# First ConvGLU tiles: where products, low parts, raw weights and one PSUM bank are placed

## The chip, the cores and the metric

The kernel runs on one core of a Trainium2 chip. Its time is the device time of one launch in microseconds (us), and a kernel's time is the median of several launches.

## The reference, cut to what matters

One layer: S5 scan and chunked attention, an output projection, then the channel mixer (ConvGLU), which is what the change is about. 512 prompt frames and 8 x 16 sample frames make T = 640 columns; D_MODEL is 1024, D_FF is 2816.

```python
h = x + mix @ p['w_o']                       # output projection, residual
hn = rms_norm(h, p['g_ffn'])
up = hn @ p['w_up']                          # 1024 -> 2 * 2816
a, b = jnp.split(up, [D_FF], axis=-1)        # gate half and value half
c, new_conv = causal_depthwise_conv(a, conv_hist, p['conv_w'], p['conv_b'])   # width 3
out = h + (jax.nn.gelu(c) * b) @ p['w_down'] # 2816 -> 1024
```

## The kernel before

Everything is fp32, and the columns lie along the free dimension (tiles of 128 x 640). For each product of a weight and an activation the kernel keeps both as a high part (rounded to fp32r, TensorE's fast format) and a low part (the rest), and adds high x high, high x low and low x high in PSUM.

The ConvGLU starts about 480 us into the program and lasts to the end. It works on 22 tiles `f` of 128 gate and 128 value columns, in parts of 2, 4, 4, 4, 4 and 4 tiles (`PARTS`). A tile's up-projection is written as seven products on halves of the matrices (in the manner of Strassen): A11, s1, s2, A12, s3, A22, s4, where A are quarters of the weights and s are sums of quarters (`PRODUCTS`). A product has two segments of six matmuls of 128x320 each. The seven products share four PSUM banks: A11 and A12 write sS, s1 writes sP, s2 and A22 write sT, s3 and s4 write sX. So three products wait until what lay in their bank has been read: A12 for ScalarE's copy `u2 <- sS` (L1454, `u` in the trace), A22 for VectorE's sum of `u2` and sT (L1456), and s4 for VectorE's sum of sX and `u2` (L1458). VectorE then takes the gate from sT (L1356 to L1358), the convolution (L1365, L1367), ScalarE the GELU (L1370, L1371), VectorE the product of gate and value (L1380); ScalarE copies its high part (L1381) and VectorE subtracts for its low part (L1384).

From the second part on, each tile is followed by segments of the down-projection for the tiles of the part before (four of them for f = 2 to 5, eight from f = 6 on), and VectorE adds each of their results to the residual `h_` (`down_evac`, L1407). The up-projection is fed with h without its norm: the factor 1/rms (`RS`) multiplies the gate (L1357, L1358), and since the value half is not multiplied, the residual h itself is multiplied by rms (`RM`) tile by tile (L1489, eight times), so that all that is added to it has the same factor. At the very end the final norm takes the factor out again.

The weights of tile f are two raw loads of 512 KB on the SP queue: "1" (A11 and A12) and "2" (A21 and A22); a third load "d" holds down-projection weights. All three take turns in a ring of three buffers (`wr`). VectorE makes the sums (`sums_a`, L1316 and L1317, from "2" and "1"; `sums_b`, L1322 and L1323). `parts` then makes high and low parts: ScalarE writes minus the raw values into the low tile (L1297) and rounds the raw values into the high tile (L1298), whose rounding is the same with the sign turned, and GpSimd issues a DMA that adds the raw values onto the low tile (L1299). That accumulating DMA takes the sums `s` and `t` from the chip's own memory, but "a" (from "1") and "d" a second time from HBM (argument `again`). A22's parts (`gh`, `gl`) are made by ScalarE and VectorE (L1305, L1310).

The order on each engine is written out by hand: `at(position, fn)` puts work in front of the segment with that number, `prep` holds the positions for each tile, `q` is the number of the tile's first segment and `qp` that of the tile before. Each engine runs its own instructions in that order; SP's queue holds the raw loads, GpSimd's the accumulating DMAs. Positions below zero lie in the output projection before the ConvGLU, whose own weights are split by ScalarE (`wh`, L107) and VectorE (`wl`, L112).

The ends of two lists that the change touches:

```python
A.activation(lo, src, AF.Copy, scale=-1.0)
A.activation(hi, src, AF.Copy)
G.dma_start(lo, src if again is None else again, accum_op=OP.add)
...
for i in range(8):
    at((20, 26, 34, 40, 48, 54, 62, 68)[i], lambda i=i: V.tensor_tensor(h_[i], h_[i], RM, op=OP.mult))
```

Of the kernel before, what the change touches and what calls it, by code (L numbers as in the profile page):

```python
# [24 lines left out]
PARTS = (2, 4, 4, 4, 4, 4)  # L25
# [6 lines left out]
U_D = [U_F + 44]  # L32
# [11 lines left out]
def body(nc, tc, d, ctx):  # L44
# [8 lines left out]
    V, A, G, PE, S = nc.vector, nc.scalar, nc.gpsimd, nc.tensor, nc.sync  # L53
# [27 lines left out]
    RS = const.tile([128, T], F32, name="RS")  # L81
# [980 lines left out]
    n = 0  # L1062
# [32 lines left out]
    for i in range(8):  # L1095
        if i in (2, 4, 5, 6):
            p = pair()
            a = att[(2, 4, 5, 6).index(i)]
# [41 lines left out]
    h_, X = [None] * 8, [None] * 4  # L1140
# [19 lines left out]
    def mid():  # L1160
        return h2.tile([128, T], F32, tag="m", name=nm("m"), bufs=4)
# [105 lines left out]
    R = {}  # L1267
    ops = {}
    held = {}

    def load_raw(key, u, cols=slice(0, 1024)):
        if key in (("1", 0), ("2", 0)):

            R[key] = tmp[:, 1024 * (key[0] == "2"):][:, 0:1024]
            S.dma_start(R[key], d["w"][u])
            return
        n = cols.stop - cols.start
        R[key] = wp.tile([128, 1024], F32, tag="wr", bufs=3, name=nm("wr"))[:, 0:n]
        S.dma_start(R[key], d["w"][u, :, cols])

    RING = {"w": (wp, "wh", "wl", 1024, 2), "f": (wf, "fh", "fl", 1024, 2)}

    def parts(ring, key, src, again=None):

        if ring == "m":

            t = [mid().bitcast(F32R)[:, 0:512] for _ in range(4)]
            for i in range(2):
                A.activation(t[2 + i], src[:, 512 * i:512 * i + 512], AF.Copy, scale=-1.0)
                A.activation(t[i], src[:, 512 * i:512 * i + 512], AF.Copy)  # L1290
                G.dma_start(t[2 + i], src[:, 512 * i:512 * i + 512], accum_op=OP.add)
            ops[key] = [(t[0], t[2]), (t[1], t[3])]
            return
        pool, th, tl, width, bufs = RING[ring]
        n = src.shape[-1]
        hi, lo = (pool.tile([128, width], F32R, tag=t, name=nm(t), bufs=bufs)[:, 0:n] for t in (th, tl))
        A.activation(lo, src, AF.Copy, scale=-1.0)  # L1297
        A.activation(hi, src, AF.Copy)  # L1298
        G.dma_start(lo, src if again is None else again, accum_op=OP.add)  # L1299
        ops[key] = [(hi[:, c:c + 512], lo[:, c:c + 512]) for c in range(0, n, 512)]  # L1300

    def parts_g(f):
# [8 lines left out]

    ssum = {}

    def sums_a(f):
        t = fp.tile([128, 1024], F32, tag="sa", name=nm("s"), bufs=1)
        V.tensor_tensor(t[:, 0:512], R["2", f][:, 0:512], R["2", f][:, 512:1024], op=OP.add)  # L1316
        V.tensor_tensor(t[:, 512:1024], t[:, 0:512], R["1", f][:, 0:512], op=OP.add)  # L1317
        ssum["s", f] = t

    def sums_b(f):  # L1320
        t = fp.tile([128, 1024], F32, tag="sb", name=nm("s"), bufs=1)
        V.tensor_tensor(t[:, 0:512], R["1", f][:, 0:512], R["2", f][:, 0:512], op=OP.add)  # L1322
        V.tensor_tensor(t[:, 512:1024], ssum["s", f][:, 512:1024], R["1", f][:, 512:1024], op=OP.add)  # L1323
        ssum["t", f] = t


# [7 lines left out]
    def up_seg(f, n, half):  # L1334
        w, x, b = PRODUCTS[n]
        if half == 0:
            held[b] = smps(b)
        ps = held[b][:, :HT]
        kind, part = HOME[w]
        hi, lo = ops[kind, f][part]  # L1340
        for k in (2 * half, 2 * half + 1):
            xh_, xl_ = X[k][x]
            c = slice(128 * k, 128 * k + 128)
            mm(ps, hi[:, c], xh_, k == 0, False)
            mm(ps, hi[:, c], xl_, False, False)
            mm(ps, lo[:, c], xh_, False, k == 3)
# [22 lines left out]
    def gelu():  # L1369
        A.activation(g_t[:, 0:512], c_t[:, 0:512], AF.Gelu_apprx_tanh)  # L1370
        A.activation(g_t[:, 512:640].rearrange("p (n i) -> p n i", n=NS), c_sample(c_t), AF.Gelu_apprx_tanh)  # L1371

    cs = {}

    def product(f, j):
        if j < 3:
            cs[f] = (ht(F32R), ht(F32R))
        else:
            cs[f] = tuple(h2.tile([128, T], F32R, tag="m", name=nm("m"), bufs=4) for _ in range(2))
        V.tensor_tensor(g_t, g_t, b_t, op=OP.mult)  # L1380
        A.activation(cs[f][0], g_t, AF.Copy)  # L1381

    def product_lo(f):
        V.tensor_tensor(cs[f][1], g_t, cs[f][0].bitcast(F32), op=OP.subtract)  # L1384

    downs = {}

# [18 lines left out]
    def down_evac(i):  # L1406
        V.tensor_tensor(two(h_[i]), downs[i][:, :, :HT], two(h_[i]), op=OP.add)  # L1407
# [2 lines left out]

    def prep(f, q, qp):
        if f == 0:
            p = (-61, -59, -46, -44, (-42, "f"), (-36, "f"), (-8, "w"), -30, -28)
        elif f == 1:
            p = (-29, -21, -12, 8, (6, "m"), (3, "w"), (10, "f"), 12, 13)
        elif f == 2:
            p = (5, 7, 15, 20, (17, "f"), (14, "w"), (22, "m"), 26, 28)
        elif f == 3:
            p = (24, 30, 35, 37, (37, "f"), (36, "w"), (42, "f"), 40, 42)
        else:  # L1420
            e = q - qp > 18
            p = (qp - 4, qp - 2, qp + 4, qp + 6, (qp + 6, "f"), (qp + 8, "w"), (qp + (17 if e else 14), "f"),
                 qp + 12, qp + (17 if e else 13))
        u = U_F + 2 * f
        at(p[0], lambda: load_raw(("1", f), u))
        at(p[1], lambda: load_raw(("2", f), u + 1))
        at(p[2], lambda: sums_a(f))
        at(p[3], lambda: sums_b(f))
        at(p[4][0], lambda: parts(p[4][1], ("s", f), ssum["s", f]))
        at(p[5][0], lambda: parts(p[5][1], ("a", f), R["1", f], d["w"][u]))  # L1430
        at(p[6][0], lambda: parts(p[6][1], ("t", f), ssum["t", f]))
        at(p[7], lambda: parts_g(f))
        at(p[8], lambda: parts_g_lo(f))

    f0, prev, qp = 0, None, 0
    for p, nf in enumerate(PARTS):
        for j in range(nf):
            f = f0 + j
            q = len(segs)
            prep(f, q, qp)  # L1440
            qp = q
# [20 lines left out]
            e = q + 2 * (f == 0)  # L1462
# [38 lines left out]

# [7 lines left out]
    segs = ((0, SEG_A), (SEG_A, T))  # L1509
# [227 lines left out]
```

## Time and profile before

| | |
|---|---|
| median of 3 runs | 934.83 us (933.84 to 936.38) |
| profiled execution, its own time | 934.26 us |
| span of that execution, first to last instruction | 932.4 us |
| mean granted TensorE clock | 0.995 |
| busy: PE, DVE, ACT, POOL | 97 %, 67 %, 47 %, 14 % |
| SP queue's loads (hardware DMA) | 33.8 % of the 16 DMA engines' span |
| GpSimd's DMAs (software DMA) | 30.7 % |

The profile is of one execution. PE is TensorE, DVE is VectorE, ACT is ScalarE, POOL is GpSimd and SP is the queue that issues loads. L115 is the one line that issues nearly all matmuls, so its groups are told apart by their tiles: sS, sP, sT and sX are the four banks of the up-projection, pb the larger banks of the down-projection and of the output projection. An idle time in brackets is that of the engine just before the row, with the instruction that ended it.

### The profile page before, as it was taken

Reading aid. Unit: us, or ns where it says so; the run is one execution under the profiler, and the core shown is the slowest. Engines: PE = TensorE matmul, PEld = TensorE weight load, DVE = VectorE, ACT = ScalarE, POOL = GpSimd, SP = SyncE. Lnnn points to the kernel's source line nnn. Section 1 sums busy time; section 2 is a strip of 40 time slices with the busy share of each in tenths; the row PEclk is TensorE's granted clock in tenths of the full one; section 3 lists DMA queues with packets and bytes.
Section 4 is the critical chain, followed back from the end, with each engine's and each line's share of the span. In section 5 each row is a group of like instructions: output and inputs, shape, how many; then the busy total and the mean of one; then the engine's idle time right before and its main releaser. Section 6 shows DMA issues by size and latency. Waiting matters only on the chain.

```text
span 932.4 us, 16524 instructions
## 1 busy us (share of the span) xinstructions
PE 903.9 (97%) x6534; PEld 867.4 (93%) x6534; DVE 627.6 (67%) x1261; ACT 441.5 (47%) x689; POOL 135.1 (14%) x230
## 2 busy tenths in 40 slices
PE   8999999999999999999998999999999999999995
PEld 7978999987878899999998899999999999999994
DVE  6793997376676444486777887666666666667545
ACT  7144112354343554434675555544646446454531
POOL 0111402400000000000012222221222212121200
PEclk9999999999999999999999999999999999999998
DMA  6744328777566422244457689888888888898833
GB/s 228 196 147 128 116 89 69 205 241 256 172 210 209 119 88 87 72 155 122 131 107 174 142 186 207 202 188 195 186 183 202 190 190 188 184 202 189 187 55 113
DMA packets 62428, 151.76 MB, mean 163 GB/s; under 512 B 20944, under 2 KB 24208, under 8 KB 62352
## 3 DMA queue, kind: packets, MB, share of 16 engines
q1 hardware_dynamic: 45392, 95.90, 33.8%
q0 software_dynamic: 16096, 54.03, 30.7%
q8 instruction: 51, 0.84, 0.4%
q10 hardware_dynamic: 864, 0.78, 0.3%
q14 instruction: 25, 0.20, 0.1%
HBM read 114.56 MB, written 8.21 MB: 132 GB/s over the span
## 4 chain that ended last, share of the span: by engine, by line
PE 73%; DVE 10%; ACT 6%; DMA 5%; issue 4%; POOL 1%; SPq 0%; DVEq 0%; POOLq 0%; ACTq 0%
PE pb L115 40%; PE sS L115 9%; PE sT L115 8%; PE sX L115 7%; PE sP L115 5%; DMA wl<-in_w 3%; DMA o_s<-SV 2%; PE sT L746 1%; PE sX L822 1%; DVE h L1535 1%; ACT wh L107 1%; PE sS L794 1%; DVE wl L112 1%; DVE h L1209 1%; DVE sm L271 1%
## 5 line engine op out<-in xcount | busy, mean ns | idle before, releaser
L115 PE MATMUL pb<-h,wh 128*128 128x320 f32 (+2 forms) x2000 | 383.5, 312 | 5.1 <-ACT h L955 1.5
L115 PEld LDWEIGHTS pb<-h,wh 128*128 128x128 f32 x2000 | 312.4, 188 | 11.0 <-issue 3.3
L115 PE MATMUL pb<-h,wl 128*128 128x320 f32 (+2 forms) x1000 | 230.1, 309 | 0.4 <-DVE wl L112 0.4
L115 PEld LDWEIGHTS pb<-h,wl 128*128 128x128 f32 x1000 | 167.3, 188 | 0.9 <-DVE wl L112 0.7
L1299 POOL DMA_DIRECT2D fl<-s x41 | 35.8, 874 | 432.9 <-PE pb L115 251.9
L107 ACT ACTIVATE wh<-wr 128x1024 fp32r<-128x1024 f32 x50 | 52.7, 1054 | 80.4 <-PE pb L115 59.9
L112 DVE TENSOR_TENSOR wl<-wr,wh 128x1024 fp32r<-128x1024 f32 x50 | 61.1, 1222 | 39.5 <-ACT wh L107 39.4
L115 PE MATMUL sS<-h,wh 128*128 128x320 f32 x336 | 74.7, 309 | 0.0
L115 PE MATMUL sX<-h,fh 128*128 128x320 f32 x320 | 71.3, 310 | 0.0
L1297 ACT ACTIVATE fl<-s 128x1024 fp32r<-128x1024 f32 x41 | 43.3, 1057 | 55.2 <-PE sT L115 48.3
L115 PEld LDWEIGHTS sS<-h,wh 128*128 128x128 f32 x336 | 56.2, 188 | 0.0
L115 PE MATMUL sS<-h,wl 128*128 128x320 f32 x168 | 52.2, 311 | 2.9 <-DMA wl<-in_w 2.9
L115 PEld LDWEIGHTS sX<-h,fh 128*128 128x128 f32 x320 | 53.8, 189 | 0.0
L693 ACT ACTIVATE sb<-sb,mx 128x128 f32<-128x128 f32 (+4 forms) x40 | 24.2, 604 | 57.7 <-DVE mx L692 44.2
L1299 POOL DMA_DIRECT2D wl<-in_w x43 | 38.2, 889 | 86.3 <-ACT wl L1297 79.1
L1370 ACT ACTIVATE tmp<-tmp 128x512 f32<-128x512 f32 x22 | 13.9, 633 | 76.4 <-DVE tmp L1367 76.4
L115 PE MATMUL sX<-h,fl 128*128 128x320 f32 x160 | 49.5, 309 | 0.0
L1297 ACT ACTIVATE wl<-wr 128x1024 fp32r<-128x1024 f32 (+1 forms) x43 | 43.5, 1011 | 6.8 <-PE sS L115 5.7
L115 PE MATMUL sT<-h,gh 128*128 128x320 f32 x176 | 40.4, 317 | 4.9 <-DVE u L1456 4.9
L1298 ACT ACTIVATE wh<-wr 128x1024 fp32r<-128x1024 f32 (+1 forms) x43 | 43.2, 1004 | 0.0
L1298 ACT ACTIVATE fh<-s 128x1024 fp32r<-128x1024 f32 x41 | 42.9, 1046 | 0.0
L1367 DVE SCALAR_TENSOR_TENSOR tmp<-tmp,vec 128x656 f32<-128x656 f32 x44 | 39.5, 898 | 0.7
(339 smaller groups left out, 1678.3 us busy)
## 6 DMA issues: line engine op xcount, KB each, us to landing
wr<-in_w SPq DMA_DIRECT2D x112, 512.0 KB, 4.6
fl<-s POOLq DMA_DIRECT2D x41, 512.0 KB, 6.0
wl<-in_w POOLq DMA_DIRECT2D x39, 512.0 KB, 8.4
kc<-in_kc SPq DMA_DIRECT2D x16, 512.0 KB, 5.4
vc<-in_vc SPq DMA_DIRECT2D x16, 512.0 KB, 5.6
x<-in_x SPq DMA_DIRECT2D x7, 320.0 KB, 6.1
pb<-in_pbias SPq DMA_DIRECT2D x8, 256.0 KB, 5.9
h<-in_x SPq DMA_DIRECT2D x6, 320.0 KB, 4.2
```

The lines of the kernel that those rows point to most:

```text
L107: A.activation(hi, raws[u], AF.Copy)
L112: V.tensor_tensor(lo, raws[u], hi.bitcast(F32), op=OP.subtract)
L115: PE.matmul(ps, lhs, rhs, start=start, stop=stop)
L271: ops.append((cost, lambda: f(*a, **k)))
L693: A.activation(sb[:, :w], sb[:, :w], AF.Exp, bias=mx[:, 2:3], accum_out=mx[:, 3:4])
L746: PE.transpose(pt[:, k * 128:k * 128 + 128], e[:, k * 128:k * 128 + 128], ident)
L794: PE.matmul(sc[32 * n:32 * n + 32, :], QB[:, hp, 4 * g4 + n].rearrange("p a b -> p (a b)"), kc[n // 2][:, n % 2, :], start=True, stop=True ...
L1297: A.activation(lo, src, AF.Copy, scale=-1.0)
L1298: A.activation(hi, src, AF.Copy)
L1299: G.dma_start(lo, src if again is None else again, accum_op=OP.add)
L1367: V.scalar_tensor_tensor(c_t, a_t[:, j:L + j], vcol(C_CW + 3 * f + j), c_t, op0=OP.mult, op1=OP.add)
L1370: A.activation(g_t[:, 0:512], c_t[:, 0:512], AF.Gelu_apprx_tanh)
```

## The change

- `parts` no longer takes a source in HBM: every accumulating DMA reads the raw tile or the sum that ScalarE has read. With `cuts` it works in pieces; "a" of f = 3, 4, 5 is made in two halves, each with a DMA of its own.
- The raw tile "1" of f = 4 and 5 is loaded as two halves into buffers of another pool (`mid`, which holds the `m` tiles), not into the ring.
- For f = 0 and 1, A22 writes a bank of the larger kind (`bigps`, pb in the trace), not sT.
- The products of f = 0 to 5 are multiplied by RS on VectorE. The eight multiplications of h by RM move into the third part (f = 6 to 9), each three segments behind the `down_evac` of the same tile of h.
- For f = 2 to 5 the product's low part is made by a ScalarE copy with scale -1 and an accumulating DMA, in place of VectorE's subtraction.
- Positions: product and its low part one and two segments later; loads, sums and parts of f = 0, 3, 4, 5 and, by one segment, the load "1" from f = 6 on.

```diff
+        if key in (("1", 4), ("1", 5)):
+            R[key] = [mid()[:, 0:512] for _ in range(2)]
+            for i in range(2):
+                S.dma_start(R[key][i], d["w"][u, :, 512 * i:512 * i + 512])
+            return
...
-    def parts(ring, key, src, again=None):
+    def parts(ring, key, src, cuts=1):
...
-        A.activation(lo, src, AF.Copy, scale=-1.0)
-        A.activation(hi, src, AF.Copy)
-        G.dma_start(lo, src if again is None else again, accum_op=OP.add)
+        for c in (slice(i, i + n // cuts) for i in range(0, n, n // cuts)):
+            x = src[c.start // 512] if isinstance(src, list) else src[:, c]
+            A.activation(lo[:, c], x, AF.Copy, scale=-1.0)
+            A.activation(hi[:, c], x, AF.Copy)
+            G.dma_start(lo[:, c], x, accum_op=OP.add)
...
-            held[b] = smps(b)
+            held[b] = bigps()[:, 0] if w == "A22" and f < 2 else smps(b)
...
+    EARLY = sum(PARTS[:2])
...
         V.tensor_tensor(g_t, g_t, b_t, op=OP.mult)
+        if f < EARLY:
+            V.tensor_tensor(g_t, g_t, RS, op=OP.mult)
+        if 1 < f < EARLY:
+            A.activation(cs[f][1], g_t, AF.Copy, scale=-1.0)
         A.activation(cs[f][0], g_t, AF.Copy)
+        if 1 < f < EARLY:
+            G.dma_start(cs[f][1], g_t, accum_op=OP.add)
 
     def product_lo(f):
-        V.tensor_tensor(cs[f][1], g_t, cs[f][0].bitcast(F32), op=OP.subtract)
+        if not 1 < f < EARLY:
+            V.tensor_tensor(cs[f][1], g_t, cs[f][0].bitcast(F32), op=OP.subtract)
...
-            p = (-61, -59, -46, -44, (-42, "f"), (-36, "f"), (-8, "w"), -30, -28)
+            p = (-61, -59, -50, -44, (-44, "f"), (-54, "f"), (-8, "w"), -30, -28)
...
-            p = (24, 30, 35, 37, (37, "f"), (36, "w"), (42, "f"), 40, 42)
+            p = (24, 30, 35, 38, (38, "f"), (36, "w"), (42, "f"), 40, 42)
...
-            p = (qp - 4, qp - 2, qp + 4, qp + 6, (qp + 6, "f"), (qp + 8, "w"), (qp + (17 if e else 14), "f"),
+            p = (qp - 3, qp - 2, qp + 4, qp + 6, (qp + 6, "f"), (qp + 8, "w"), (qp + (17 if e else 14), "f"),
                  qp + 12, qp + (17 if e else 13))
+            if f < 6:
+                p = (43 if f == 4 else 54, 44 if f == 4 else 58) + p[2:]
...
-        at(p[5][0], lambda: parts(p[5][1], ("a", f), R["1", f], d["w"][u]))
+        at(p[5][0], lambda: parts(p[5][1], ("a", f), R["1", f], 2 if 2 < f < 6 else 1))
...
-            at(e + 17, lambda f=f, j=j: product(f, j))
-            at(e + 18, lambda f=f: product_lo(f))
+            at(e + 18, lambda f=f, j=j: product(f, j))
+            at(e + 20, lambda f=f: product_lo(f))
...
+                    if p == 2:
+                        at(len(segs) + 3, lambda i=i: V.tensor_tensor(h_[i], h_[i], RM, op=OP.mult))
...
-    for i in range(8):
-        at((20, 26, 34, 40, 48, 54, 62, 68)[i], lambda i=i: V.tensor_tensor(h_[i], h_[i], RM, op=OP.mult))
```

Three places show what moves. Line numbers from 1274 on are shifted in the changed program: L1380 becomes L1392, L1384 L1403, L1322 L1333, L1323 L1334, L1455 L1476, L1456 L1477, L1458 L1479, L1454 L1475, L1381 L1397, L1297 L1304 and L1298 L1305. First VectorE behind the GELU of f = 0, while TensorE works on f = 1; before:

```order
L1380 TENSOR_TENSOR tmp<-tmp 128x640
L1384 TENSOR_TENSOR h_5529<-tmp,h_5528 128x640
L1322 TENSOR_TENSOR s_5539<-wr_5352,wr_5377 128x512
L1323 TENSOR_TENSOR s_5539<-s_5481,wr_5352 128x512
L1489 TENSOR_TENSOR h_4735<-h_4735,RM 128x640
L1455 TENSOR_TENSOR tmp<-sS_5545,u_4663 128x320
L1456 TENSOR_TENSOR u_4663<-sT_5521,u_4663 128x320
L1458 TENSOR_TENSOR tmp<-sX_5570,u_4663 128x320
```

and in the changed program:

```order
L1392 TENSOR_TENSOR tmp<-tmp 128x640
L1394 TENSOR_TENSOR tmp<-tmp,RS 128x640
L1333 TENSOR_TENSOR s_5539<-wr_5352,wr_5377 128x512
L1334 TENSOR_TENSOR s_5539<-s_5481,wr_5352 128x512
L1403 TENSOR_TENSOR h_5535<-tmp,h_5534 128x640
L1476 TENSOR_TENSOR tmp<-sS_5544,u_4663 128x320
L1477 TENSOR_TENSOR u_4663<-sT_5521,u_4663 128x320
L1479 TENSOR_TENSOR tmp<-sX_5570,u_4663 128x320
```

One multiplication stands for another (RS for RM), and the low part (L1403) has gone from the second place to behind the sums.

Second ScalarE between the GELU of f = 2 and the copy that frees bank sS for A12 of f = 3; before:

```order
L1370 ACTIVATE tmp<-tmp 128x512
L1371 ACTIVATE tmp<-tmp 128x128
L1381 ACTIVATE h_5806<-tmp 128x640
L1297 ACTIVATE wl_5826<-wr_5738 128x512
L1298 ACTIVATE wh_5825<-wr_5738 128x512
L1454 ACTIVATE u_4663<-sS_5818 128x320
```

and in the changed program:

```order
L1381 ACTIVATE tmp<-tmp 128x512
L1382 ACTIVATE tmp<-tmp 128x128
L1396 ACTIVATE h_5816<-tmp 128x640
L1397 ACTIVATE h_5815<-tmp 128x640
L1304 ACTIVATE wl_5831<-wr_5740 128x512
L1305 ACTIVATE wh_5830<-wr_5740 128x512
L1475 ACTIVATE u_4663<-sS_5823 128x320
```

One copy (L1396, the one with scale -1) has come in ahead of it.

Third the SP queue, the three raw loads ("d", "1", "2") that are issued in one tile from f = 7 on, with the semaphores that each waits for (DMASW are those of GpSimd's DMAs, DMAHW those of the loads before it); before:

```order
L1279 DMA wr_6494<-in_w 128x1024 [waits DMAHW0_49,Activation_49]
L1279 DMA wr_6528<-in_w 128x1024 [waits DMAHW1_49,DVE_49,Activation_49]
L1279 DMA wr_6543<-in_w 128x1024 [waits DMAHW2_49,DVE_49,Activation_49]
```

and in the changed program:

```order
L1284 DMA wr_6509<-in_w 128x1024 [waits DMAHW2_49,DMASW0_49,Activation_49]
L1284 DMA wr_6549<-in_w 128x1024 [waits DMASW2_49,DMAHW3_49,DVE_49,Activation_49]
L1284 DMA wr_6558<-in_w 128x1024 [waits DMAHW4_49,DVE_49]
```

"d" and "1" now wait for one of GpSimd's accumulating DMAs as well; "2" does not.

## Rows read from the trace of the kernel before

**Rows 1.** By stretch: length, busy PE, PEld, DVE, ACT, POOL, clock, DMA share, GB/s.

```profile
500.00:520.00 20.00, 16.02 (x97) 15.76 (x98) 15.91 (x28) 9.78 (x15) 5.77 (x9) 0.91 0.54 122
...
580.00:620.00 40.00, 40.00 (x275) 40.00 (x274) 27.96 (x46) 22.05 (x29) 9.07 (x15) 1.00 0.83 188
```

**Rows 2.** What PE waited for, 440 to 932 us: total, times, longest.

```profile
PE sT L115 <- DVE u L1456: 4.9, 3, 2.9
PE sS L115 <- DMA wl<-in_w: 2.9, 3, 2.0
...
PE pb L115 <- DVE h L1407: 0.8, 1, 0.8
PE pb L115 <- ACT wh L107: 0.6, 1, 0.6
...
PE pb L115 <- DVE wl L112: 0.4, 1, 0.4
```

**Rows 3.** Timeline of ACT in the output projection: start, length, idle before.

```profile
431.64 0.83 ACT L1197 ACTIVATE m<-h,vec 128x640 f32<-128x640 f32 x1 [3.54 <-DVE h L1209]
...
443.83 1.05 ACT L1297 ACTIVATE fl<-tmp 128x1024 fp32r<-128x1024 f32 x1
...
448.07 0.83 ACT L1197 ACTIVATE m<-h,vec 128x640 f32<-128x640 f32 x1 [1.62 <-DVE h L1209]
```

**Rows 4.** Timeline of DVE, 497 to 503 us (f = 1).

```profile
497.37 0.83 DVE L1380 TENSOR_TENSOR tmp<-tmp 128x640 f32<-128x640 f32 x1 [2.57 <-ACT tmp L1371]
499.00 0.82 DVE L1384 TENSOR_TENSOR h<-tmp,h 128x640 fp32r<-128x640 f32 x1 [0.81 <-ACT h L1381]
...
502.80 0.49 DVE L1458 TENSOR_TENSOR tmp<-sX,u 128x320 f32<-128x320 f32 x1
```

**Rows 5.** Timeline of PE, 499 to 506 us (f = 1: end of s3, A22, s4).

```profile
499.55 0.31 PE L115 MATMUL sX<-h,fl 128*128 128x320 f32 x1
...
502.75 0.68 PE L115 MATMUL sT<-h,gh 128*128 128x320 f32 x2 [2.89 <-DVE u L1456]
...
505.89 0.72 PE L115 MATMUL sX<-h,fh 128*128 128x320 f32 x2
```

**Rows 6.** Timelines of ACT and of PE at A12 of f = 3.

```profile
529.49 0.42 ACT L1454 ACTIVATE u<-sS 128x320 f32<-128x320 f32 x1
...
530.53 0.46 PE L115 MATMUL sS<-h,wh 128*128 128x320 f32 x2
```

**Rows 7.** DMA issues of 580 to 880 us: number, KB, median us to landing.

```profile
wr<-in_w SPq DMA_DIRECT2D x47, 512.0 KB, 7.8
wl<-in_w POOLq DMA_DIRECT2D x32, 512.0 KB, 8.7
fl<-s POOLq DMA_DIRECT2D x30, 512.0 KB, 5.8
```

**Rows 8.** DMAs issued at 598.5, 599.2 and 614.5 us.

```profile
wl<-in_w POOLq DMA_DIRECT2D x1, 512.0 KB, 10.5
wr<-in_w SPq DMA_DIRECT2D x1, 512.0 KB, 10.0
...
wr<-in_w SPq DMA_DIRECT2D x1, 512.0 KB, 3.6
```

**Rows 9.** One tile in the steady run, 605 to 626 us: POOL, DVE and PE.

```profile
605.68 0.88 POOL L1299 DMA_DIRECT2D wl<-in_w  x1 [1.03 <-ACT wl L1297]
...
613.77 0.69 DVE L1310 TENSOR_TENSOR gl<-wr,gh 128x512 fp32r<-128x512 f32 x1
...
618.24 0.69 DVE L1316 TENSOR_TENSOR s<-wr 128x512 f32<-128x512 f32 x1 [0.92 <-DMA wr<-in_w]
...
621.12 0.69 DVE L1322 TENSOR_TENSOR s<-wr,wr 128x512 f32<-128x512 f32 x1 [1.46 <-DMA fl<-s]
...
623.61 0.49 DVE L1455 TENSOR_TENSOR tmp<-sS,u 128x320 f32<-128x320 f32 x1 [1.19 <-PE sS L115]
...
625.10 0.46 PE L115 MATMUL sT<-h,gh 128*128 128x320 f32 x2
```

More of the change, by code (lines that the diff above doesn't have):

```diff
@@ L1294, in parts @@
         pool, th, tl, width, bufs = RING[ring]
-        n = src.shape[-1]
+        n = 1024 if isinstance(src, list) else src.shape[-1]
         hi, lo = (pool.tile([128, width], F32R, tag=t, name=nm(t), bufs=bufs)[:, 0:n] for t in (th, tl))
-        A.activation(lo, src, AF.Copy, scale=-1.0)
-        A.activation(hi, src, AF.Copy)
-        G.dma_start(lo, src if again is None else again, accum_op=OP.add)
+        for c in (slice(i, i + n // cuts) for i in range(0, n, n // cuts)):
[3 more added lines that the diff above has]
+            G.dma_start(lo[:, c], x, accum_op=OP.add)
         ops[key] = [(hi[:, c:c + 512], lo[:, c:c + 512]) for c in range(0, n, 512)]
@@ L1312, in body, with upper @@
     ssum = {}
+    def upper(f):
+        r = R["1", f]
+        return r if isinstance(r, list) else [r[:, 0:512], r[:, 512:1024]]
     def sums_a(f):
@@ L1316, in sums_a @@
         V.tensor_tensor(t[:, 0:512], R["2", f][:, 0:512], R["2", f][:, 512:1024], op=OP.add)
-        V.tensor_tensor(t[:, 512:1024], t[:, 0:512], R["1", f][:, 0:512], op=OP.add)
+        V.tensor_tensor(t[:, 512:1024], t[:, 0:512], upper(f)[0], op=OP.add)
         ssum["s", f] = t
@@ L1321, in sums_b @@
         t = fp.tile([128, 1024], F32, tag="sb", name=nm("s"), bufs=1)
-        V.tensor_tensor(t[:, 0:512], R["1", f][:, 0:512], R["2", f][:, 0:512], op=OP.add)
-        V.tensor_tensor(t[:, 512:1024], ssum["s", f][:, 512:1024], R["1", f][:, 512:1024], op=OP.add)
+        V.tensor_tensor(t[:, 0:512], upper(f)[0], R["2", f][:, 0:512], op=OP.add)
+        V.tensor_tensor(t[:, 512:1024], ssum["s", f][:, 512:1024], upper(f)[1], op=OP.add)
         ssum["t", f] = t
@@ L1476, in body @@
                 at(q - 7 if f > 2 else 20, lambda f=f, u=u, cols=cols: load_raw(("d", f), u, cols))
-                at(q + 1 if f > 2 else 23, lambda f=f, u=u, cols=cols: parts("w", ("d", f), R["d", f],
-                                                                             d["w"][u, :, cols]))
+                at(q + 1 if f > 2 else 23, lambda f=f, u=u, cols=cols: parts("w", ("d", f), R["d", f]))
                 for o in range(per):
@@ L1497, in body @@
         at(lp, lambda n=n: load_raw(("x", n), U_D[-2] + n))
-        at(pr, lambda n=n, ring=ring: parts(ring, ("x", n), R["x", n], d["w"][U_D[-2] + n]))
+        at(pr, lambda n=n, ring=ring: parts(ring, ("x", n), R["x", n]))
         for o in range(2):
```

## The prediction

> **What bounds the kernel now.** I read the busy time by stretch first, then PE's waits, then the timelines at the places that the waits name. In the steady run from f = 7 on PE is busy 40.00 of 40.00 us at the full clock, while DVE and ACT are busy 28 and 22 of 40 [rows 1]: there nothing can be gained, only lost. The stretch of 500 to 520 us is another matter: PE is busy 16.02 of 20 and the granted clock falls to 0.91 [rows 1]. From 440 us on PE waits 4.9 us in three places for `u2` (L1456) before A22, 2.9 us in three places for A11's low part, 0.8 us for the last `down_evac`, and 0.6 and 0.4 us for a weight's parts in the output projection [rows 2]; so the change can reach 9.6 us of idle time, and what the clock cost. A wait costs PE a little more than its row says: the last matmul issued before the gap at f = 1 started at 499.55 and lasts 0.31 [rows 5], but the next could have been issued 0.15 behind its start (275 matmuls in 40.00 us [rows 1]), so 0.16 us come on top of each gap.
>
> **The change part by part,** against the profiled execution's own 934.26 us (its span is 932.4). The median of the runs, 934.83, lies 0.57 above it, and I add that at the end.
>
> *Output projection.* The wait of 1.0 us in all [rows 2] stands at the end of a chain: ACT makes "a" of f = 0 in two instructions of 1.05 us (the first at 443.83), and behind them VectorE's sum comes late, so that ACT itself stands idle 1.62 us for it before L1197 at 448.07 [rows 3]. They move 18 segments up, to where ACT stands idle 3.54 us before L1197 at 431.64 [rows 3], which covers both. I take -1.0; without that cover it is 0.
>
> *f = 1.* A22 now writes another bank and can start at 499.70 (499.55 + 0.15 [rows 5]); its 12 matmuls end at 501.45. Then s4 still needs sX read by L1458, which starts at 502.80 [rows 4]. Ahead of it VectorE has as many instructions as before (RS for RM, both 128x640), but the 0.81 us that L1384 waits for ACT's copy [rows 4] are now filled by the sums: the product starts at 497.37 and takes 0.83 [rows 4], the one with RS as long again, the copy about 0.8 (L1197 has the same size [rows 3]), so it is ready at 499.8, while the two sums keep VectorE beyond 500. So L1458 starts at 502.0 and s4 at 502.5. Before, s4 starts at 505.89 [rows 5], for A22 ran from 502.75 to there, 3.1 us for what takes 1.75 at the full clock: the gap of 2.89 [rows 5] had brought the clock down. The gain is 3.4, of which 1.4 is the clock; a wait of about 1.0 us stays, now on sX. If the shorter gap brings the clock down too, some 1.4 comes back.
>
> *f = 2.* A22 writes sT as before, and the chain product, RS, copy, low part, sums, L1455, L1456 is as long as with RM: the wait stays. Its raw tiles may come later, since their ring buffers are now held until an accumulating DMA has landed. Bounds: 0.2 less (VectorE loses an instruction earlier on) to 2 more (half of a load of 3.6 [rows 8]). I take +0.3, near the lower end, for the sums did not wait here before.
>
> *f = 3.* The low part leaves VectorE (0.82 [rows 4] and the wait for ACT's copy), so the wait on L1456 goes. (Of the 4.9 us, 2.9 are f = 1; the other two make 2.0 together [rows 2], and I share them out as 1.2 for f = 2 and 0.8 for f = 3, whose sums are ready sooner.) But ACT gets a second copy and starts later behind the RS product: up to 0.83 + 0.8. The copy `u2 <- sS` ends at 529.91 and A12 starts at 530.53 [rows 6]: 0.6 of room, so up to 1.0 of new wait. I take 0.75: no change, -0.05.
>
> *f = 4 to 6.* A11's low part comes from the chip, in halves for f = 4 and 5, of which A11 needs the first. From 580 us on accumulating DMAs out of HBM take 8.7 us in the median, those out of the chip's memory 5.8 [rows 7]: 2.9 sooner, against waits of 2.0 at most [rows 2]. They go, -2.9; ACT's longer chain takes 0.5 back over the three tiles (0 to 1). -2.4.
>
> *Steady run.* Bytes go down, but raw "d" and "1" now wait for the landing of their accumulating DMAs, and "2" stands behind "1" in SP's queue, so that VectorE's sums, then s, t and all products wait for it. "a" is issued at 605.68 [rows 9]; at 5.8 it lands at 611.5 and "1" is issued. "2" can't be issued before VectorE has made `gl`, at 614.5 (613.77 + 0.69 [rows 9]), so it isn't late as long as "a" takes under 8.8. Then "2" takes 3.6 [rows 8] and the sums start at 618.2, as now [rows 9]. Room behind them: VectorE waits 1.19 for PE before L1455, and L1455 and L1456, 0.5 each, are done 0.45 before A22 at 625.10 [rows 9]: 1.6. The multiplications by RM put two instructions of 0.8 into each of f = 6 to 9; before them 1.46 of waiting on L1322 for a DMA [rows 9] cover them nearly. I take 0; it is the dear place if I am wrong.
>
> *Tail.* `down_evac` for the first bank no longer stands behind the last low part: -0.8.
>
> *Gaps themselves.* Six go (two in the output projection, three on DMAs, the tail), A22's at f = 1 and 3 become others, one comes new at f = 6: five by 0.16, -0.8.
>
> Sum: -1.0 - 3.4 + 0.3 - 0.05 - 2.4 - 0.8 - 0.8 = -8.15, so 926.1, and with 0.57 the forecast is 926.7. With all costs at their good ends: -1.0 - 3.6 - 0.2 - 0.8 - 2.9 - 0.8 - 0.8 = -10.1, 924.7. With the bad ones (output projection 0, the clock's 1.4 back, f = 2 at +2, f = 3 at +0.2, f = 4 to 6 at -1.9, tail and gaps -1.2): -2.9, 931.9.
>
> **The rivals.**
>
> *Loads become the loop of the steady run (slower).* 15 tiles, f = 7 to 21, each need "a" landed before "1" and "2" of the next. Accumulates beside a load have been slow: one issued at 598.5 took 10.5 and the load issued 0.7 later took 10.0, both landing together [rows 8]. "Through the chip's memory" halves HBM traffic but not the DMA engines' work (share 0.83 [rows 1]). The point from which it decides: "2" landing 1.6 late, 5.2 after its issue. At "a" 8.7 and "2" 7.8, the medians of now [rows 7], it lands at 622.3, 4.2 late, 2.6 over the room: 39 us in 15 tiles. Halfway ("a" 7.3, "2" 5.7) it is 2.1 late, 0.5 over: 7.5. I price it at 0.8 a tile, 12 us: 938.7. Against it: loads held back are loads that no longer run beside the accumulate that they wait for.
>
> The Trainium skill, "DMA: Bandwidth & Descriptors", section "Queues, rings and completion order", says that each DMA engine takes the queues that have work in turn, packet by packet. That agrees with the pair that landed together [rows 8]; the load issued at 614.5, though, took 3.6 with t's accumulate issued behind it, as if alone. In the changed order t's parts stand ahead of the product's copy on ACT, so that t's accumulate moves up beside "2". By the rule "2" then needs up to twice its 3.6, lands 2.0 beyond the room, and 15 tiles cost 30 us, 956.7; by the row it costs nothing.
>
> *The first tiles give back what they gain (still faster, by less).* Raw loads behind accumulates at f = 2 to 6, ACT's chain of f = 3 to 6: the bad ends above, 931.9; I give it 930 to 933.
>
> *It does not do what it says.* If accumulates out of the chip's memory take as long as those out of HBM, the 2.9 stay: 929.8, inside the former.
>
> **How the numbers follow.** Forecast (924.7 to 929.5): 0.58. First tiles give back (929.5 to 933): 0.16. Loop late, any size: 0.22, of which the sharing rule 0.04. More gain than the good ends: 0.04. A measurement here tells 0.3 % from no change, 2.8 us. Faster than 932.0: 0.58 + 0.04 + 0.09 of the second case = 0.71. Within: 0.07 of it and 0.03 of a small loop, 0.10. Slower than 937.6: 0.19. The range leaves out 0.02 below and, above, the loop from 0.8 a tile on: 924 to 938.5; the forecast's own is 924.7 to 929.5.
>
> **What would show it.** Right: no wait on wh or wl at the end of the output projection; at f = 1 one short gap before sX released by L1479 and no clock below full; at f = 2 a gap of about 1.2 before sT; at f = 3 a gap before A12 released by ACT's copy from sS; none on DMA before A11; PE busy 40.00 of 40.00 from 600 on. Wrong: gaps before sT in every tile from f = 7 on, with the first sum waiting for a raw load; or raw loads late at f = 2 to 6.

## The result, and the profile after

The changed kernel takes 929.37 us in the median of 12 runs (927.54 to 934.2), the kernel before 935.61 beside it; the ratio is 0.9945 (95 % interval 0.9929 to 0.9961), so 5 us, 0.55 %, are gained where 8.15 were forecast. Two of the 12 runs of the kernel before were slow ones (988 and 1186 us), and the ratios here and below leave such runs out. The profiled execution takes 928.25 us with a span of 926.5, against 934.26 and 932.4: 6.0 less.

What PE waited for in the changed kernel, 470 to 930 us (total, times, longest), answers to [rows 2]:

```profile
PE sT L115 <- DVE u L1477: 3.6, 3, 1.6
...
PE sS L115 <- ACT u L1475: 1.1, 2, 0.6
PE sX L115 <- DVE tmp L1479: 1.0, 1, 1.0
```

No wait on a DMA before A11 or on `down_evac` is left, and PE's timeline shows none on `wh` or `wl` in the output projection. Between f = 1 and 900 us it has these gaps (start, length, idle before, releaser); they stand at f = 1, 2, 3, twice at f = 6, and at f = 7:

```profile
500.85 0.56 PE L115 MATMUL sX<-h,fh 128*128 128x320 f32 x2 [0.96 <-DVE tmp L1479]
...
513.24 0.56 PE L115 MATMUL sT<-h,gh 128*128 128x320 f32 x2 [1.56 <-DVE u L1477]
...
526.30 0.56 PE L115 MATMUL sS<-h,wh 128*128 128x320 f32 x2 [0.48 <-ACT u L1475]
...
574.95 0.56 PE L115 MATMUL sS<-h,wh 128*128 128x320 f32 x2 [0.64 <-ACT u L1475]
579.40 0.57 PE L115 MATMUL sT<-h,gh 128*128 128x320 f32 x2 [0.67 <-DVE u L1477]
...
600.39 0.57 PE L115 MATMUL sT<-h,gh 128*128 128x320 f32 x2 [1.36 <-DVE u L1477]
```

The first four were forecast, as 1.0, 1.5, 0.75 and 0.5. The last two were not. By stretch (columns as in [rows 1]) the clock stays full at 500 to 520, and PE loses 2.3 us from 560 to 600:

```profile
500.00:520.00 20.00, 17.59 (x118) 17.32 (x119) 17.30 (x32) 10.45 (x17) 6.61 (x12) 1.00 0.82 191
...
560.00:600.00 40.00, 37.73 (x254) 36.90 (x252) 27.52 (x46) 21.30 (x28) 9.03 (x16) 1.00 0.91 198
...
840.00:880.00 40.00, 40.00 (x275) 40.00 (x274) 23.84 (x39) 21.10 (x28) 8.60 (x14) 1.00 0.82 191
```

What those two gaps wait for is seen on VectorE, whose first sum for the next tile stands still for a raw load:

```profile
575.80 0.69 DVE L1327 TENSOR_TENSOR s<-wr 128x512 f32<-128x512 f32 x1 [3.84 <-DMA wr<-in_w]
...
596.78 0.69 DVE L1327 TENSOR_TENSOR s<-wr 128x512 f32<-128x512 f32 x1 [4.32 <-DMA wr<-in_w]
```

The four DMAs ahead of the first of them, issued at 561.6 ("a" of f = 6), 562.6 ("d"), 569.1 ("1") and 569.6 us ("2" of f = 7), took (KB, us to landing):

```profile
wl<-wr POOLq DMA_DIRECT2D x1, 512.0 KB, 7.4
wr<-in_w SPq DMA_DIRECT2D x1, 512.0 KB, 6.6
wr<-in_w SPq DMA_DIRECT2D x1, 512.0 KB, 5.3
wr<-in_w SPq DMA_DIRECT2D x1, 512.0 KB, 6.1
```

"a" lands at 569.0, beside a "d" that was itself held back; only then does SP issue "1", 0.4 us later "2", which lands at 575.7. At f = 7 it is the same again; "a" issued at 580.6, "1" at 589.1 and "2" at 589.5 took

```profile
wl<-wr POOLq DMA_DIRECT2D x1, 512.0 KB, 8.4
wr<-in_w SPq DMA_DIRECT2D x1, 512.0 KB, 6.2
wr<-in_w SPq DMA_DIRECT2D x1, 512.0 KB, 7.2
```

From the next tile on this fits: at 613.9 the sum waits 0.44 for its load, and PE has no gap up to 880.

Term by term, from the two profiled executions:

| step | forecast | measured |
|---|---|---|
| output projection, with its gaps' own cost | -1.3 | the ConvGLU's first gap (A12 of f = 0) ends at 480.44 in place of 482.15: -1.7 (in the mean of nine profiles with the move and four without: 480.41 and 481.89, -1.5) |
| f = 1, from there to the start of s4 | -3.4 | 20.41 in place of 23.74: -3.3 |
| f = 2, gap | +0.3 | 1.23 to 1.56: +0.3 |
| f = 3, gap | -0.05 | 0.80 to 0.48: -0.3 |
| f = 4 to 6, gaps before A11 and A12 | -2.4 | 2.92 to 0.64: -2.3 |
| f = 6 on, gaps before A22 | 0 | 0.67 + 1.36: +2.0 |
| tail | -0.8 | -0.8 |

The other 0.5 us of the forecast, the own cost of three more gaps, has no row of its own here.

### The profile page after: what moved, and what is told of

Read it like the earlier page. It is cut to its first block, busy times and chain, and to the rows that moved or that the text cites. A ratio compares the mean times of both kernels' runs of the same rounds, so it can differ in the third digit from the quotient of the medians.

```text
span 926.5 us, 16572 instructions
## 1 busy us (share of the span) xinstructions
PE 902.5 (97%) x6534; PEld 866.0 (93%) x6534; DVE 629.3 (68%) x1263; ACT 443.3 (48%) x699; POOL 139.6 (15%) x237
## 4 chain that ended last, share of the span: by engine, by line
PE 73%; DVE 12%; issue 6%; ACT 5%; DMA 2%; POOL 2%; SPq 0%; DVEq 0%; POOLq 0%; ACTq 0%
PE pb L115 41%; PE sS L115 9%; PE sX L115 7%; PE sT L115 7%; PE sP L115 5%; DMA wr<-in_w 2%; PE sT L746 1%; PE sX L822 1%; POOL ks L531 1%; DVE tmp L1378 1%; DVE wl L112 1%; DVE h L1556 1%; ACT wh L107 1%; PE sS L794 1%; DVE h L1209 1%
## 5 line engine op out<-in xcount | busy, mean ns | idle before, releaser
L1304 ACT ACTIVATE fl<-s 128x1024 fp32r<-128x1024 f32 x41 | 43.4, 1057 | 51.1 <-PE sT L115 38.9
L1304 ACT ACTIVATE wl<-wr 128x1024 fp32r<-128x1024 f32 (+1 forms) x42 | 41.6, 991 | 20.5 <-PE pb L115 15.7
L1306 POOL DMA_DIRECT2D wl<-wr x42 | 36.6, 872 | 89.1 <-ACT wl L1304 88.9
L1381 ACT ACTIVATE tmp<-tmp 128x512 f32<-128x512 f32 x22 | 13.9, 633 | 75.0 <-DVE tmp L1378 71.5
L1305 ACT ACTIVATE fh<-s 128x1024 fp32r<-128x1024 f32 x41 | 42.9, 1046 | 0.0
L1305 ACT ACTIVATE wh<-wr 128x1024 fp32r<-128x1024 f32 (+1 forms) x42 | 41.2, 981 | 0.0
L115 PE MATMUL sT<-h,gh 128*128 128x320 f32 x160 | 35.8, 311 | 3.6 <-DVE u L1477 3.6
```

The lines of the kernel that those rows point to most:

```text
L115: PE.matmul(ps, lhs, rhs, start=start, stop=stop)
L1304: A.activation(lo[:, c], x, AF.Copy, scale=-1.0)
L1305: A.activation(hi[:, c], x, AF.Copy)
L1306: G.dma_start(lo[:, c], x, accum_op=OP.add)
```

## The experiments

Times are those of the profiled execution, beside 928.25 for the changed kernel, with the ratio to the kernel before that ran beside each. Six undo a part of the change (e1 to e6), two apply a part alone (e8, e9), the others are versions that these pointed to.

**e1: A22 of f = 0 and 1 in bank sT again.**

```diff
-            held[b] = bigps()[:, 0] if w == "A22" and f < 2 else smps(b)
+            held[b] = smps(b)
```

> The changed kernel with one edit taken back: A22 of f = 0 and 1 writes bank sT again. Theory (the bank was worth its wait and the clock): at f = 1 A22 stands before L1477, which ends at 500.2 in the changed kernel's trace while PE is free at 498.2, so a gap of about 2.0 us before sT in place of 0.96 before sX; s4 then starts 1.2 us later than with the edit, and 1.4 us more if the granted clock falls again as it did behind the gap of 2.89. Against the changed kernel's 928.25 us: 929.4 without the clock, 930.8 with it. Rival (the gain at f = 1 came from VectorE's order, RS for RM and the sums ahead of the low part, and the wait would only have been on sX): within 0.3 us of the changed kernel, no gap over 1.2 at f = 1.

931.15 us, ratio 0.9972 (0.9958 to 0.9986). PE's timeline at f = 1:

```profile
499.78 0.56 PE L115 MATMUL sT<-h,gh 128*128 128x320 f32 x2 [2.12 <-DVE u L1477]
...
501.64 0.46 PE L115 MATMUL sX<-h,fh 128*128 128x320 f32 x2
```

The gap is 2.12, A22 then runs 1.86 us at the full clock, and s4 starts 21.67 behind A12 of f = 0 (479.97) in place of 20.41: +1.3. The theory holds, without the clock. Not all of it stays lost: at f = 2 the gap is 1.09 in place of 1.56. The other 1.6 us of this execution lie elsewhere: gaps before A22 at 737.6, 757.9 and 855.1, of 1.68, 0.53 and 0.20, again with VectorE waiting for a raw load.

**e9: that bank alone, in the kernel before:**

```diff
-            held[b] = smps(b)
+            held[b] = bigps()[:, 0] if w == "A22" and f < 2 else smps(b)
```

> The kernel before with one part of the change alone: A22 of f = 0 and 1 writes a larger bank. Theory: at f = 1 the gap of 2.89 before sT becomes one of 1.7 to 1.8 before sX (L1458 ends at 503.29, A22 fills 1.75), and the clock stays full: s4 starts at 503.4 in place of 505.89, -2.5 us against 934.26. Rival (the clock falls behind any gap over a microsecond or two): 1.0 to 1.4 of it stays lost, -1.1 to -1.5.

930.98 us, ratio 0.9984 (0.9972 to 0.9996).

```profile
502.92 0.57 PE L115 MATMUL sX<-h,fh 128*128 128x320 f32 x2 [1.73 <-DVE tmp L1458]
```

The gap is the one forecast, the clock stays full, and s4 starts 21.19 us behind A12 of f = 0 in place of 23.74: 2.55 sooner, as the theory has it. Over all runs 0.4 to 2.6 us are left of that. With e1 the 3.3 us won at f = 1 come apart, though not into a sum: the bank alone wins 2.55, VectorE's order without the bank 2.1 (21.67 in e1 in place of 23.74), and in both the clock stays full, so either of them wins back the clock's 1.4.

**e3: the old positions of f = 0.**

```diff
-            p = (-61, -59, -50, -44, (-44, "f"), (-54, "f"), (-8, "w"), -30, -28)
+            p = (-61, -59, -46, -44, (-42, "f"), (-36, "f"), (-8, "w"), -30, -28)
```

> The changed kernel with the old positions of f = 0 (parts of 'a' at -36, sums at -46, parts of 's' at -42). Theory (two ACT instructions of 1.05 us there delay VectorE's sum and so the weight behind it): the gaps before wh and wl in the output projection come back, 0.6 + 0.4 and 0.3 for starting again, +1.0 to +1.4 us against 928.25. Rival (they went because something else moved, or it would show up again as a longer wait at the start of the ConvGLU): within 0.3.

```profile
452.21 0.85 PE L115 MATMUL pb<-h,wh 128*128 128x320 f32 x4 [0.63 <-ACT wh L107]
453.48 0.55 PE L115 MATMUL pb<-h,wl 128*128 128x320 f32 x2 [0.41 <-DVE wl L112]
```

Both gaps are back and the ConvGLU is 1.34 us later (481.78): the theory. The gaps show it better than the time, for in e6, which has neither gap, the ConvGLU is late by as much as 1.04 (481.48). The execution as a whole took 936.04, and the runs spread from 928.76 to 939.37 (ratio 0.9988, 0.9966 to 1.001), for this one has late loads at 738.5, 760.7 and 859.9, gaps of 1.31, 2.39 and 0.53.

**e4: low parts of the products of f = 2 to 5 on VectorE again.**

```diff
-        if 1 < f < EARLY:
-            A.activation(cs[f][1], g_t, AF.Copy, scale=-1.0)
...
-        if 1 < f < EARLY:
-            G.dma_start(cs[f][1], g_t, accum_op=OP.add)
...
-        if not 1 < f < EARLY:
-            V.tensor_tensor(cs[f][1], g_t, cs[f][0].bitcast(F32), op=OP.subtract)
+        V.tensor_tensor(cs[f][1], g_t, cs[f][0].bitcast(F32), op=OP.subtract)
```

> The changed kernel with the low parts of the products of f = 2 to 5 subtracted on VectorE again (no copy with scale -1, no accumulating DMA for them). Theory (the second copy on ACT is what A12 of f = 3 and 6 waits for): the gaps of 0.48 and 0.64 us before sS go, while VectorE's low part and its wait for ACT's copy, 0.8 + 0.9, lie ahead of the sums again, so that A22 of f = 3 waits for L1477 by up to 0.8, and f = 4 and 5 little or nothing: between -1.0 and +0.6 against 928.25. Rival (the copies of 'd' on ACT are the wait, not the second copy): both gaps before sS stay and gaps before sT come on top, +0.8 to +2.5.

930.64 us, ratio 0.9955 (0.9939 to 0.9971). Both gaps before sS are gone, and none before sT came at f = 3: the second copy on ACT was the wait, and for sT at f = 3 to 5 taking it to ACT was not needed. But the gap before sT at f = 6 grew from 0.67 to 1.26: the late load came only 0.4 sooner (the sum behind it starts at 575.38 in place of 575.80), and PE 1.0. 1.05 us in two more gaps lie at 756 and 854. The time missed its range: 2.4 us over the changed kernel, where -1.0 to +0.6 was expected. These gaps and a ConvGLU that starts 0.4 later do not account for all of it, and over all runs the two kernels are not told apart (0.9955 and 0.9945).

**e2: all accumulating DMAs of "a" and "d" from HBM again.**

```diff
-    def parts(ring, key, src, cuts=1):
+    def parts(ring, key, src, cuts=1, again=None):
...
-            G.dma_start(lo[:, c], x, accum_op=OP.add)
+            G.dma_start(lo[:, c], x if again is None else again[:, c], accum_op=OP.add)
...
-        at(p[5][0], lambda: parts(p[5][1], ("a", f), R["1", f], 2 if 2 < f < 6 else 1))
+        at(p[5][0], lambda: parts(p[5][1], ("a", f), R["1", f], 2 if 2 < f < 6 else 1, d["w"][u]))
...
-                at(q + 1 if f > 2 else 23, lambda f=f, u=u, cols=cols: parts("w", ("d", f), R["d", f]))
+                at(q + 1 if f > 2 else 23, lambda f=f, u=u, cols=cols: parts("w", ("d", f), R["d", f], 1, d["w"][u, :, cols]))
```

> The changed kernel with the accumulating DMAs of 'a' and 'd' reading HBM again (halves, positions and banks as changed). Theory (the gaps of 0.67 and 1.36 us before sT at f = 6 and 7 come from raw buffers held until the accumulate lands, so that '2' of the next tile is late): both gaps go, VectorE's first sum there no longer waits 3.8 and 4.3 us for a raw load, -2.3 us; and some of the 2.9 us on A11's low part at f = 4 to 6 come back, 0.5 to 2.9, since the halves alone may be enough for f = 4 and 5. Sum between -1.8 and +0.6 against 928.25. Rival (those gaps come from the later products or from the RM multiplications on VectorE): both gaps stay, and the DMA waits come on top, +0.5 to +2.9.

928.82 us, ratio 0.9949 (0.9932 to 0.9966): no difference from the changed kernel. The two gaps before sT are gone, PE has none from 580 to 880, and a new one stands before A11 of f = 6, whose low part is a whole 512 KB; f = 4 and 5, in halves, have none (at f = 4 the first half lands at 536.9, before A11's first low part at 537.26, and the second at 538.5):

```profile
571.77 0.64 PE L115 MATMUL sS<-h,wl 128*128 128x320 f32 x1 [2.48 <-DMA wl<-in_w]
```

So reading on the chip trades this wait for late loads. The RM multiplications and the later products are still there, so the rival falls. The medians of 600 to 880 us, changed kernel first, then e2, show both sides: accumulating DMAs out of the raw tile are 1.1 us shorter and loads 1.8, but those out of the sums are 1.7 longer, and the loads start later.

```profile
wr<-in_w SPq DMA_DIRECT2D x43, 512.0 KB, 4.8
wl<-wr POOLq DMA_DIRECT2D x29, 512.0 KB, 6.7
fl<-s POOLq DMA_DIRECT2D x28, 512.0 KB, 6.5
```

```profile
wr<-in_w SPq DMA_DIRECT2D x43, 512.0 KB, 6.6
wl<-in_w POOLq DMA_DIRECT2D x28, 512.0 KB, 7.8
fl<-s POOLq DMA_DIRECT2D x27, 512.0 KB, 4.8
```

**e8: on-chip sources alone, in the kernel before;** the call for "a" stands for all three:

```diff
-        at(p[5][0], lambda: parts(p[5][1], ("a", f), R["1", f], d["w"][u]))
+        at(p[5][0], lambda: parts(p[5][1], ("a", f), R["1", f]))
```

> The kernel before with one part of the change alone: all accumulating DMAs read the raw tile on the chip. Theory (that swaps DMA waits before A11 for late raw loads): the waits on 'a' at f = 4 to 6 shrink from 2.9 to 0 to 1.5 us, and gaps before sT, with VectorE's first sum waiting for a raw load, appear at one to several tiles from f = 4 on, 0.3 to 2 us each: between 932 and 938 for the profiled execution against 934.26. Rival (less HBM traffic makes every DMA shorter and nothing is late): no new gap before sT, 931 to 932.

938.66 us, ratio 1.0032 (1.0019 to 1.0045): slower. The waits before A11 are gone; new or longer gaps before sT came, the longest two 2.02 (f = 3) and 2.87 (f = 4):

```profile
536.18 0.56 PE L115 MATMUL sT<-h,gh 128*128 128x320 f32 x2 [2.02 <-DVE u L1456]
555.15 0.56 PE L115 MATMUL sT<-h,gh 128*128 128x320 f32 x2 [2.87 <-DVE u L1456]
```

with VectorE waiting for the load before the second of them:

```profile
550.81 0.69 DVE L1316 TENSOR_TENSOR s<-wr 128x512 f32<-128x512 f32 x1 [3.16 <-DMA wr<-in_w]
```

The clock fell behind the second one (last section), which adds to the loss. Less HBM traffic did not make everything earlier; the rival falls.

**e5 and e6: one of the two from HBM** ("a" in e5, "d" in e6; e2's edit with `again` in one call).

> The changed kernel with only the accumulating DMAs of 'a' reading HBM again; 'd' still reads its raw tile. Theory (raw '1' held until its accumulate has landed makes '1' and '2' of the next tile late, as both are issued only behind it): no gap before sT at f = 6 and 7 nor anywhere from 580 to 880 us, and A11 of f = 6 waits for its low part by 1 to 2.5 us; 927 to 929.5 for the profiled execution against 928.25. Rival (held 'd' is what does it: its late load runs beside the accumulates of 's' and 'a'): the gaps before sT at f = 6 and 7 stay, 0.5 to 1.4 us each.

> The changed kernel with only the accumulating DMAs of 'd' reading HBM again; 'a' still reads its raw tile. Theory (held '1' makes the loads late): the gaps before sT at f = 6 and 7 stay, 0.5 to 1.4 us each, and single ones may come later. Rival (held 'd' makes them late): both go, 926 to 926.5 against 928.25, with no DMA wait before A11.

e5: 925.63 us, ratio 0.9919 (0.9903 to 0.9935). No gap before sT from f = 3 on; A11 of f = 6 waits 0.49, less than expected, and that of f = 4 0.15. e6: 928.45 us, ratio 0.9923 (0.9907 to 0.9939). The gap at f = 6 is gone (A11 there waits 0.51 instead), the one at f = 7 stays:

```profile
600.64 0.56 PE L115 MATMUL sT<-h,gh 128*128 128x320 f32 x2 [1.11 <-DVE u L1477]
```

So the held "1" is enough to make a load late, at f = 7, and the held "d" beside it makes it worse; the held "d" alone makes none late enough to stop PE. e5's time is below the range expected for it, since so little came back before A11. e5's profile has 2.0 us fewer in gaps before sT; that its runs are below the changed kernel's, by 0.26 % of two ratios whose intervals overlap at their ends, agrees with that.

**e10: A22 of f = 2 in the larger bank too.**

```diff
-            held[b] = bigps()[:, 0] if w == "A22" and f < 2 else smps(b)
+            held[b] = bigps()[:, 0] if w == "A22" and f < 3 else smps(b)
```

> The changed kernel with A22 of f = 2 in the larger bank as well. Theory: the gap of 1.56 before sT at f = 2 becomes 0.4 before sX: -1.2 us against 928.25. Rival (the down-projection of f = 2 needs the two larger banks, and its first segments wait for the gate to read A22's): a gap before pb of 0.5 to 1.5 us at f = 2 in its place, -0.7 to +0.3.

929.17 us, ratio 0.9942 (0.9926 to 0.9958): nothing gained, and not for the rival's reason. The gap at f = 2 is 0.40 before sX, as forecast, but the next one, on ACT's copy, takes up the rest:

```profile
526.04 0.56 PE L115 MATMUL sS<-h,wh 128*128 128x320 f32 x2 [1.65 <-ACT u L1475]
```

It was 0.48. That copy starts at 525.57, in the changed kernel at 525.84, with a ConvGLU 0.27 earlier: ACT's chain (GELU, product on VectorE, two copies, parts of "d") did not move, so PE meets it sooner and waits for the difference.

**e7 and e11: a combination, run twice.** "a" and "d" from HBM, "1" of f = 6 in halves as well (below), e10's bank and e4's edit. The rows are of e11.

```diff
-        if key in (("1", 4), ("1", 5)):
+        if key in (("1", 4), ("1", 5), ("1", 6)):
...
-        at(p[5][0], lambda: parts(p[5][1], ("a", f), R["1", f], 2 if 2 < f < 6 else 1))
+        at(p[5][0], lambda: parts(p[5][1], ("a", f), R["1", f], 2 if 2 < f < 7 else 1, d["w"][u]))
```

> The changed kernel with what the earlier runs point to: accumulates of 'a' and 'd' read HBM again (raw buffers free early), '1' of f = 6 also in halves in the other pool (its first half lands before A11), A22 of f = 2 in the larger bank too, low parts of the products of f = 2 to 5 on VectorE. Theory: the gap of 1.56 before sT at f = 2 becomes one of about 0.4 before sX (L1479 stands 0.6 behind L1477, and A22 takes 1.75), -1.2; the gaps of 0.48 and 0.64 before sS go, -1.1; those of 0.67 and 1.36 before sT go, -2.0; five gaps by 0.16, -0.6: 923.4 to 924.5 against 928.25 for the profiled execution, ratio to the kernel before about 0.990. Rival (gaps come back elsewhere, at A22 of f = 3 or at A11 of f = 6, since VectorE's low part and HBM's accumulates are late there): 926 to 929.

> The combined kernel once more, for a profile in an undisturbed execution: 923 to 925. Theory: no gap before sS or sT from f = 2 on, the one before sX of f = 2 about 0.4, that of f = 1 still 0.96, no DMA wait over 0.5 before A11 of f = 6, nothing from 580 to 880. Rival: a DMA wait of 1 to 2.5 before A11 of f = 4, 5 or 6, since 'a' and 'd' both come from HBM.

Ratios 0.9885 (0.9868 to 0.9903) and 0.9904 (0.9888 to 0.992), 924.36 us in e11's profile: faster than both kernels, by 4 to 6 us against the changed one. At f = 2 the gap is 0.39; those before sS and sT are gone; 580 to 880 us are full:

```profile
580.00:880.00 300.00, 300.00 (x2045) 299.96 (x2044) 202.74 (x329) 157.66 (x201) 63.18 (x109) 1.00 0.87 191
```

One wait that nobody expected came at f = 3, where PE, now earlier, meets the low part of `s`:

```profile
522.61 0.41 PE L115 MATMUL sP<-h,fl 128*128 128x320 f32 x1 [1.49 <-DMA fl<-s]
```

**e12: the combination with "d" from the chip and "1" of f = 6 in the ring.**

> The combined kernel with two differences: 'd' keeps its raw tile as source, and '1' of f = 6 stays in the ring. Theory (one of the two sources on the chip is enough to keep A11's wait short, and 'a' from HBM is enough to keep the loads early): as e11 within 0.7 us, with a DMA wait of 0.3 to 0.6 before A11 of f = 6. Rival (the halves of f = 6 are needed): a wait of 1 to 2.5 there, 925 to 927.

927.92 us, ratio 0.9928 (0.9911 to 0.9946): the rival.

```profile
571.14 0.42 PE L115 MATMUL sS<-h,wl 128*128 128x320 f32 x1 [1.79 <-DMA wl<-in_w]
```

A11 of f = 6 waits 1.79 for its low part, where e5 had 0.49 with the same two sources. PE comes to it only 0.2 sooner, counted from A12 of f = 0, for a new wait of 1.69 at f = 3 (on the low part of `s`, as in e11) stands in place of e5's gaps of 1.56 and 0.32; most of the difference is the DMA, which took 9.3 us in place of 8.1. The source of "d" is not what does it, since e2, with "d" from HBM, waits 2.48 there. So at f = 6 "1" in halves in the other pool is needed; whether it is the halves or the pool that helps, no run tells apart.

## Why the prediction was right, and where it was not

The direction and the time were right: 929.4 for 926.7, just inside the forecast's own range, which ends at 929.5. The steps at f = 1, 2, 4 to 6 and the tail came within some 0.1 us of their terms. e1 and e9 show the step at f = 1 separately, and e3 the one in the output projection. The place at the edge of the range has luck in it: the output projection and f = 3 gave 0.2 to 0.4 and 0.3 more than their terms, and without that the 2.0 of the next paragraph would have carried the time out of it.

*What failed* is the step of the steady run, "I take 0; it is the dear place if I am wrong": +2.0 us, and with it nearly all of the difference between 8.15 and 6.0. The sum used there has "2" issued 8.8 behind "a" and landed 3.6 later, 7.0 before A22 at 625.10, with 1.6 of room [rows 8, rows 9]. In the changed kernel "a" of f = 6 and 7 is issued at

```profile
561.63 0.86 POOL L1306 DMA_DIRECT2D wl<-wr  x1 [1.03 <-ACT wl L1304]
580.55 0.86 POOL L1306 DMA_DIRECT2D wl<-wr  x1 [1.04 <-ACT wl L1304]
```

It took 7.4 and 8.4, not 5.8, and "2" was issued 7.9 and 8.9 behind it, about as the sum has it. What the sum had wrong is the load: "2" left right behind "1", and beside it took 6.1 and 7.2, not 3.6. Besides, "a" of f = 6 is issued 17.1 before PE is ready for A22 (16.6 in the kernel before), where the row used, of f = 8, has 19.4. So "2" landed only 3.0 and 2.3 before PE was ready for A22. From f = 8 on "2" takes 4.6 to 5.4 and lands 5.6 to 6.6 before A22 (f = 8 to 13); that is enough, but at its least it leaves 0.2 of the 1.6. The rival had the mechanism and too high a price: it was late in two tiles of 15 in the profiled execution, not in all. Undoing it (e2, e5) removes both gaps; applying it alone (e8) makes the kernel slower.

*Right for less than the reason given:* f = 4 to 6. The 2.9 us were put down to the shorter accumulate out of the chip's memory. e2 has the HBM source and no wait at f = 4 and 5: there the halves are what matters, since A11 needs only the first. At f = 5 the two halves even took longer out of the chip's memory (7.4 and 7.7) than out of HBM (6.7 and 6.9 in e2). At f = 6, which is not cut, the source matters. f = 2 is such a case too: its term allowed for late raw tiles, but no sum there waits for a load; VectorE's chain to L1477 is 0.2 longer.

*The clock's 1.4 us* at f = 1 was right: gaps of 0.96, 1.73 and 2.12 at that place left it full. That a shorter gap is safe does not follow: in e12 the clock fell behind one of 1.79 (last section).

*The sharing rule* was given 0.04 and a price of 30 us. The tiles f = 6 and 7 fit it: there t's accumulate is issued ahead of both loads, while in tile f = 8, the third row, it comes behind "1", which leaves at 608.1:

```profile
566.87 0.86 POOL L1306 DMA_DIRECT2D fl<-s  x1 [1.37 <-ACT fl L1304]
588.00 0.86 POOL L1306 DMA_DIRECT2D fl<-s  x1 [4.78 <-ACT fl L1304]
609.00 0.86 POOL L1306 DMA_DIRECT2D fl<-s  x1 [4.79 <-ACT fl L1304]
```

"1" took 5.3 and 6.2 in the first two, and 3.4 to 3.7 from f = 8 on. But "2" is lengthened by 1.0 to 1.8 from f = 8 on, not by 3.6, so PE does not lose 2 us in every tile: it is full from 620 to 880. How much of it is "1" beside "2", and how much t's accumulate, is not told apart.

*Open:* in the profiles of e1, e3, e4, e8 and e10, all with both sources on the chip, single late loads come back between 737 and 860 us, at nearly the same places (737.6, 738.5; 757.9, 760.7, 755.9, 755.8; 855 to 860, 853.9, 853.1; that of e8 stands at 783.8), none in the changed kernel's own profile, nor in e2, e5, e6, e11 and e12. What sets them off was not tried; the little room that is left from f = 8 on would let a small delay show, which is argued and not shown. They may be why the gain over all runs is 5.1 us, not 6.0.

## What to carry to other kernels

A buffer that a transfer still reads is a buffer that a load can't have: price a change of source by when the buffer comes free, not only by the bytes it saves. A wait taken away is worth only the distance to the next chain that did not move (e10: ACT's copy; e4, e11 and e12: DMAs), so take the waits of several tiles together, or list the next one before counting the gain. Where only the first part of a transfer is needed first, cutting it in two may do more than making it faster. The price of a load is that of a load beside what will run next to it: take it from such a row, and look at the first tile of a run of tiles as well as at one in the middle.

## What the runs showed of the hardware

TensorE's granted clock fell from the upper of its two levels, 2.4 GHz, to the lower, 1.2 (0.50 from 502.5 to 506.5 us in e8), behind gaps of 1.79 (e12), 2.39 (e3), 2.48 (e2), 2.87 (e8) and 2.89 us (before, e8), in stretches around them that read 0.61 to 0.91; it stayed full behind those of 2.12 (e1), 2.02 (e8), 1.99 (before) and 1.76 and 1.73 (e9). So a gap's length alone does not tell in these profiles whether the clock falls. The first row is of e12 around its gap, the second of the kernel before around that of 1.99; then e2, and e8 around 2.02 and 2.87:

```profile
568.00:580.00 12.00, 10.21 (x60) 9.94 (x59) 7.38 (x11) 5.80 (x9) 1.53 (x2) 0.86 0.86 208
540.00:552.00 12.00, 10.01 (x68) 9.75 (x68) 9.29 (x14) 6.01 (x10) 2.50 (x3) 1.00 0.84 208
```

```profile
566.00:580.00 14.00, 11.52 (x70) 11.26 (x69) 8.31 (x12) 7.70 (x11) 2.88 (x4) 0.88 0.96 224
```

```profile
530.00:542.00 12.00, 9.98 (x69) 9.72 (x67) 9.89 (x19) 6.54 (x7) 3.16 (x7) 1.00 0.68 139
552.00:560.00 8.00, 5.13 (x24) 4.87 (x24) 6.31 (x13) 4.53 (x5) 2.32 (x5) 0.79 0.75 156
```

An accumulating DMA that reads the chip's own memory was shorter in the steady run than one from HBM, but not by one amount: 6.7 against 7.8 in the medians of the changed kernel and e2, 5.0 ("d") against 8.3 ("a") inside e5. And the kernel that reads 91.5 MB from HBM in place of 114.6 keeps the DMA engines nearly as busy: 0.84 of the time from 600 to 880 us, against 0.86 before.
